# The attention gate folded into the output projection's weights, and the residual added where the partial projection is made

## The chip, the cores and the metric

The kernel runs on one core of a Trainium2 chip. The time is the device time of one execution in microseconds (us). The engines are TensorE (PE, with its weight loads listed apart as PEld), VectorE (DVE), ScalarE (ACT), GpSimd (POOL) and SyncE (SP). SP issues nearly all the DMA transfers, in its own order; an instruction on SP that must wait for a tile holds up everything behind it.

## The reference, cut to what matters

One encoder layer with 1024 positions, model width 1024, 8 latent-attention (MLA) heads and 8 chunked-attention heads of width 64, and a gated MLP of width 2816, all in float32. `g_a`, the attention gate, has one value for each output column and is the same for all positions.

```python
mod = jnp.dot(jax.nn.silu(c), w_ada[l]) + b_ada[l]
sh_a, sc_a, g_a, sh_m, sc_m, g_m = jnp.split(mod, N_MOD, axis=-1)
h = modulate(rmsnorm(x, g_attn_norm[l]), sh_a, sc_a)
...
o_mla = mla_attention(q, k, v)
...
o_ca = chunk_attention(cq, ck, cv, rel_bias[l])
mixed = jnp.dot(jnp.concatenate([o_mla, o_ca], axis=-1), w_out[l])
x = x + g_a[:, None, :] * mixed
h = modulate(rmsnorm(x, g_mlp_norm[l]), sh_m, sc_m)
u = causal_dwconv(jnp.dot(h, w_up[l]), conv_w[l], conv_b[l])
gate, val = jnp.split(u, 2, axis=-1)
x = x + g_m[:, None, :] * jnp.dot(jax.nn.silu(gate) * val, w_down[l])
```

## The kernel before

Every float32 operand of a large product is split into a high part (`hi_of`, line 77 when ACT makes it) and a low part (`lo_of`, line 84, a subtraction on POOL or DVE), and `gemm3` makes three matmuls of each pair: lines 154, 155 and 156. An engine letter chooses who splits: "a" is ACT, "p" POOL, "v" DVE.

The work runs in this order.

1. Up to about 400 us: the modulation vectors, the first norm, the input projection, and the chunked heads. Each head is a unit of four or eight query tiles. For each tile PE makes scores (L765 or L771), DVE masks and takes their minimum (the scores carry a minus sign; L789, L790), ACT exponentiates (L797), DVE takes the reciprocal of the sum (L799, L800), POOL makes a float16 high part (L73) and DVE the low part (L819), SP issues a transposing DMA (L831, tile `PTm` for the latent heads), and PE multiplies by the values (L859) into `pvm`. ACT and DVE together scale the result into `om` (L868, L869), and SP stores it to `oT_d` in DRAM (L873).
2. About 400 to 627 us: the latent heads, by the same steps. Between the tiles' matmuls other work is interleaved (`pace` and `fill_step` take it from the list `fillers`). The last filler is `f_oca`, the chunked heads' half of the output projection: it loads four 128x512 blocks of `w_out` for each half of the columns (`load_wo`), then for each of the 8 row tiles loads the heads' output `cl` and, for each half of the columns, runs 12 matmuls into a PSUM tile `oc`; ACT copies that into a tile `co` (L686; two buffers, tag "sq") and SP stores it to `part_d` (L687).
3. A side filler, `f_ada`, computes the remaining modulation vectors. It leaves the attention gate, spread over all 128 partitions, in DRAM as `ga_d`, long before `f_oca`.
4. About 627 to 722 us: the latent heads' half of the projection. For each row tile 24 matmuls go into `op` (two PSUM banks; three such tiles), with `oh` and `ol` (the heads' output, `o_load`) against `wo` (the other four blocks of `w_out`, from `load_wo` again). DVE then adds the partial sum (L1141), multiplies by the gate `gabc` (L1142), adds x (L1143); SP stores `x1_d`; ACT squares for the norm (L1145), POOL finishes the mean (L119, L120), DVE scales (L1150). PE transposes the rows (`mod_T`, L1044), ACT applies scale and shift (`hv`, L1046), and `bpage` and lines 1179 to 1199 make the differences and splits `b..` and `t..` that the MLP's products use (L1075, L1082 to L1084).
5. From about 722 us: the up-projection by a Strassen-like scheme, convolution, gate and down-projection, to the end at 1344 us.

The order of instructions on each engine is not that of the text: a planner in the framework simulates the program with its own costs and priorities and writes each engine's order (the heads have a high priority; `issue_after` adds constraints). So a change in the text also moves instructions it doesn't name. An engine executes its order strictly.

`load_wo` takes its raw tiles from a pool with tag "A" and five buffers (`atile`), shared with `f_ada`; a tile's buffer comes free when its last reader is done. For `f_oca` both halves are split by ACT and POOL. The late call is `wo = [load_wo(0, n, "a", "v" if n else "p") for n in range(2)]`: the second half's low parts are made by DVE.

Of the kernel before, what the change touches and what calls it, by code (L numbers as in the profile page):

```python
# [13 lines left out]
F32 = mybir.dt.float32  # L14
# [4 lines left out]
AF = mybir.ActivationFunctionType  # L19
# [3 lines left out]
MUL, ADD, SUB, MIN, MAX = ALU.mult, ALU.add, ALU.subtract, ALU.min, ALU.max  # L23

P = 128
D = 1024
# [38 lines left out]
def layer_kernel(ctx, tc, I, out):  # L65
    nc = tc.nc
    pe, act, dve, pool, sp = nc.tensor, nc.scalar, nc.vector, nc.gpsimd, nc.sync

    def f32(ap):
        return ap.bitcast(F32)  # L70
# [4 lines left out]
    def hi_of(eng, o, i):  # L75
        if eng == "a":
            act.activation(o, i, AF.Copy)  # L77
        elif eng == "p":
            pool.tensor_scalar(o, i, 1.0, 0.0, op0=MUL, op1=ADD)
        else:  # L80
            dve.tensor_copy(o, i)

    def lo_of(eng, o, i, hi):
        (pool if eng == "p" else dve).tensor_tensor(o, i, f32(hi), op=SUB)  # L84
# [4 lines left out]
    part_d = dram.tile([NT, P, D], F32, name="part_d")  # L89
    ga_d = dram.tile([P, D], F32, name="ga_d")  # L90
# [24 lines left out]
    anchor = {}  # L115

    def rsqrt_mean(r, ss, n, cols=None):
        sc = ss if cols is None else ss[:, cols]
        pool.tensor_scalar(sc, sc, 1.0 / n, EPS, op0=MUL, op1=ADD)  # L119
        anchor["r"] = pool.tensor_tensor(r, ss, nhalf[:].to_broadcast(list(r.shape)), op=ALU.pow).ins  # L120
# [17 lines left out]
    def rtile(name, shape=(P, 512), dt=F32):  # L138
        return apg.tile(list(shape), dt, name=name, tag="R", bufs=4)

    def qtile(name):
        return apg.tile([P, 512], F32, name=name, tag="sq", bufs=2)

    def atile(name):
        return apg.tile([P, 512], F32, name=name, tag="A", bufs=5)
# [4 lines left out]
    def gemm3(pt, pairs, start=True, stop=True):  # L150

        n = len(pairs)
        for i, (sh, sl, mh, ml) in enumerate(pairs):
            pe.matmul(pt, sh, mh, start=(start and i == 0), stop=False)  # L154
            pe.matmul(pt, sh, ml, start=False, stop=False)  # L155
            last = pe.matmul(pt, sl, mh, start=False, stop=(stop and i == n - 1))  # L156
        anchor["pe"] = last.ins
# [5 lines left out]
    def gemm3_f(pt, pairs, step=GSTEP):  # L163
        n, w = len(pairs), pt.shape[-1]
        for i0 in range(0, n, step):
            part = pairs[i0:i0 + step]
            if len(trail) > LAG:
                with tc.issue_after(trail[-1 - LAG]):
                    gemm3(pt, part, i0 == 0, i0 + step >= n)
            else:  # L170
                gemm3(pt, part, i0 == 0, i0 + step >= n)
            yield 3 * len(part) * max(107, w / 2.4 + 2.5)
# [104 lines left out]
    for d in range(ND):  # L277
# [7 lines left out]
        pt = ps.tile([P, 512], F32, name=f"p_ada{d}", tag="mm", bufs=2)  # L285
# [14 lines left out]
        for t in range(NT):  # L300
            h, j = divmod(t, 4)
            sl = slice(j * P, (j + 1) * P)
# [285 lines left out]
    def g4(shape, dt, name):  # L588
        return G["4"].tile(shape, dt, name=name, tag="G4", bufs=8)
# [71 lines left out]

    def load_wo(k0, n, he, le):
        ws = []
        for k in range(k0, k0 + 4):
            raw = atile(f"wor{k}_{n}")
            sl = slice(n * 512, (n + 1) * 512)
            sp.dma_start(raw[:], I["w_out"][k * P:(k + 1) * P, sl])
            w = g4([P, 2, 512], F32R, f"wo{k}_{n}")
            hi_of(he, w[:, 0], raw[:])
            lo_of(le, w[:, 1], raw[:], w[:, 0])  # L670
            ws.append(w)
        return ws

    def f_oca():
        ws = [load_wo(4, n, "a", "p") for n in range(2)]
        for t in range(NT):
            lo = rtile(f"cl{t}", (P, 4, P), F32R)
            hi = rtile(f"ch{t}", (P, 4, P), F32R)
            sp.dma_start(f32(lo[:]), oT_d[4:8, :, t * P:(t + 1) * P].rearrange("k p t -> p k t"))
            hi_of("a", hi[:], f32(lo[:]))  # L680
            lo_of("p", lo[:], f32(lo[:]), hi[:])
            for n in range(2):
                pt = ps.tile([P, 512], F32, name=f"oc{t}_{n}", tag="mm", bufs=2)
                yield from gemm3_f(pt[:], [(hi[:, k], lo[:, k], ws[n][k][:, 0], ws[n][k][:, 1]) for k in range(4)])
                o = qtile(f"co{t}_{n}")
                act.activation(o[:], pt[:], AF.Copy)  # L686
                sp.dma_start(part_d[t][:, n * 512:(n + 1) * 512], o[:])  # L687


# [322 lines left out]
    oh, ol, ox = {}, {}, {}  # L1012

    def o_load(t):
        ol[t] = go.tile([P, 4, P], F32R, name=f"ol{t}", tag="ol", bufs=4)
        oh[t] = go.tile([P, 4, P], F32R, name=f"oh{t}", tag="oh", bufs=4)
        anchor["ol"] = sp.dma_start(f32(ol[t][:]), oT_d[0:4, :, t * P:(t + 1) * P].rearrange("k p t -> p k t")).ins
        hi_of("a", oh[t][:], f32(ol[t][:]))
        lo_of("p", ol[t][:], f32(ol[t][:]), oh[t][:])
# [9 lines left out]
    gb = gbp.__enter__()  # L1029
# [11 lines left out]
    def mod_T(k, h):  # L1041
        pt = ps2.tile([P, 512], F32, name=f"ht_ps2_{k}_{h}", tag="hT", bufs=2)
        for j in range(4):
            pe.transpose(pt[:, j * P:(j + 1) * P], xn2[4 * h + j][:, k * P:(k + 1) * P], ident[:])  # L1044
        v = tb.tile([P, 512], F32, name=f"hv2_{k}_{h}", tag="v", bufs=13)
        act.activation(v[:], pt[:], AF.Identity, scale=modT[:, 2, k:k + 1], bias=modT[:, 3, k:k + 1])  # L1046
        return v

    def bpage(nm, k, v, le):
        pg = hpools[(nm, k)] if (nm, k) in hpools else h2p.tile([P, 2, 512], F32R, name=f"{nm}_{k}")  # L1050
        hi_of("a", pg[:, 0], v[:])
        lo_of(le, pg[:, 1], v[:], pg[:, 0])
        B[nm, k] = pg
# [1 line left out]
    r2 = cst.tile([P, NT], F32, name="r2")  # L1055
    xn2 = {}
    cvp = xp.tile([P, NC_PACK - C_CV], F32, name="cvp")
    gabc = gb.tile([P, D], F32, name="gabc")
    def mt(tag, shape, name, dt=F32):
        return mp["a" if tag in ("raw", "w2", "ws") else "b"].tile(list(shape), dt, name=name, tag=tag, bufs=MB[tag])  # L1060

# [47 lines left out]
        w.append(split(a12, f"wg{j}"))  # L1109
        return w  # L1110

    op_ = {t: gb.tile([P, D], F32, name=f"pa{t}", tag="pa", bufs=4) for t in range(4)}

    def x_load(t):
        if t > 3:
            op_[t] = gb.tile([P, D], F32, name=f"pa{t}", tag="pa", bufs=4)
        sp.dma_start(op_[t][:], part_d[t])
        if t not in ox:
            ox[t] = tb.tile([P, D], F32, name=f"x1_{t}", tag="x1", bufs=8)
        with tc.issue_after(anchor["ol"]):  # L1120
            anchor["wu"] = sp.dma_start(ox[t][:], I["x"][t * P:(t + 1) * P, :]).ins

    ox[7] = tb.tile([P, D], F32, name="x1_7", tag="x1", bufs=8)
    sp.dma_start(gabc[:], ga_d[:])
    for t in range(2):
        x_load(t)
    raw0, wa0, wb0 = ff_load(0)
# [5 lines left out]
    for t in range(NT):  # L1133
        pt = ps2.tile([P, 1024], F32, name=f"op{t}", tag="op", bufs=3)
        for n in range(2):
            gemm3(pt[:, n * 512:(n + 1) * 512],
                  [(oh[t][:, k], ol[t][:, k], wo[n][k][:, 0], wo[n][k][:, 1]) for k in range(4)])
        if t + 4 < NT:
            o_load(t + 4)
        pa, x1 = op_[t], ox[t]  # L1140
        dve.tensor_tensor(pa[:], pa[:], pt[:], op=ADD)  # L1141
        dve.tensor_tensor(pa[:], pa[:], gabc[:], op=MUL)  # L1142
        dve.tensor_tensor(x1[:], x1[:], pa[:], op=ADD)  # L1143
        sp.dma_start(x1_d[t], x1[:])
        act.activation(pa[:], x1[:], AF.Square, accum_out=ss2[:, t:t + 1])  # L1145
        if t + 4 < NT:
            x_load(t + 4)
        rsqrt_mean(r2[:, t:t + 1], ss2[:, t:t + 1], D)
        xn2[t] = x1
        dve.tensor_scalar(x1[:], x1[:], r2[:, t:t + 1], 1.0, op0=MUL, op1=MUL)  # L1150
        if t == 4:
            for k in range(ND):
                v0[k] = mod_T(k, 0)
                bpage("b11" if k < 4 else "b21", k % 4, v0[k], "v" if k % 2 else "p")
# [371 lines left out]
    for t in range(4):  # L1526
        o = dl.tile([P, 512], F32, name=f"oe{t}", tag="oe", bufs=3)
# [62 lines left out]
def build(arrays):  # L1590
    nc = bacc.Bacc("TRN2", target_bir_lowering=False, num_devices=1, dynamic_dma_scratch_size=1024)
    I = {k: nc.dram_tensor(k, v.shape, mybir.dt.from_np(v.dtype), kind="ExternalInput").ap()
         for k, v in arrays.items()}
    out = nc.dram_tensor("out_0_dram", (S, D), F32, kind="ExternalOutput").ap()
    with tile.TileContext(nc, schedule_with_timeline_sim=True) as tc, ExitStack() as ctx:
        layer_kernel(ctx, tc, I, out)
    return nc
# [8 lines left out]
```

## Time and profile before

| | us |
|---|---|
| median of 3 runs (lowest, highest) | 1341.02 (1340.53, 1343.16) |
| the profiled execution | 1345.89 |
| its span in the trace | 1344.1 |
| PE busy | 1223.8 |
| DVE busy | 1096.2 |
| ACT busy | 622.7 |
| POOL busy | 578.1 |

The mean granted TensorE clock of that execution is 0.946. In the rows quoted below, a group of instructions is written as line, engine, operation, output and inputs, shape and count, then the total busy time, the mean ns of one, and the idle time of the engine just before them with what ended most of it. A row of waits is the engine and line that waited, what it waited for, the total in us, how many times, and the longest. A row of windows has the stretch, its length, the busy time of each engine with the count of instructions, the granted clock (1.00 is full), the share of the DMA engines' time and the GB/s. Chain and timeline rows begin with start and duration. A tile's rows give the minimum, median and maximum ns of one instruction, and the starts of the first and the last.

### The profile page before, as it was taken

To read this page: it belongs to the slowest core of one execution; us is meant where nothing else is said; L and a number is where in the kernel's file an instruction comes from. 1 tells how busy PE (TensorE), PEld (TensorE's weight loads), DVE (VectorE), ACT (ScalarE), POOL (GpSimd) and SP (SyncE) were. 2 spreads that over 40 slices of the span, in tenths; PEclk is the share of its full clock that TensorE was granted. 3 is DMA by queue.
4 is the path that set the end of the run, shared out by engine and by line. 5 is a ranking of instruction groups with operands and counts; after the bars stand their busy time and mean duration, and the time that the engine had idled before them with its cause. 6 is when DMAs were issued, how large, how long until landed. Compare 5 with 4: busy or idle time off the path is not lost.

```text
span 1344.1 us, 18696 instructions
## 1 busy us (share of the span) xinstructions
PE 1223.8 (91%) x6168; PEld 1003.8 (75%) x6168; DVE 1096.2 (82%) x1928; ACT 622.7 (46%) x1132; POOL 578.1 (43%) x610
## 2 busy tenths in 40 slices
PE   4899798998877798886998999999999998999998
PEld 3788587896655567765776888888888886888886
DVE  6978798864679987894989988988899997687667
ACT  4453546443555544563376444444434444433431
POOL 5464557565646763354634444444445431000000
PEclk9899798998787889996999999999999998999999
DMA  8415577854413477779911333333323326943441
GB/s 323 138 35 116 135 177 179 192 127 110 87 32 80 94 153 165 141 150 252 377 49 47 126 110 133 103 122 98 133 102 118 126 98 241 390 141 117 130 161 63
DMA packets 223689, 190.57 MB, mean 142 GB/s; under 512 B 148708, under 2 KB 166884, under 8 KB 223592
## 3 DMA queue, kind: packets, MB, share of 16 engines
q1 hardware_dynamic: 223592, 189.38, 49.1%
q8 instruction: 48, 0.79, 0.2%
q14 instruction: 49, 0.40, 0.1%
HBM read 117.24 MB, written 37.49 MB: 115 GB/s over the span
## 4 chain that ended last, share of the span: by engine, by line
PE 41%; DVE 10%; issue 3%; ACT 2%; DMA 1%; POOL 1%; SPq 0%; DVEq 0%; ACTq 0%; POOLq 0%
PE p L1082 7%; PE p L1084 7%; PE p L1083 7%; PE dnA_P L1417 2%; PE dnA_P L1419 2%; PE dnA_P L1418 2%; PE dnB_P L1419 1%; PE dnB_P L1418 1%; PE dnB_P L1417 1%; DVE u L1253 1%; DVE u L1254 1%; PE op L154 1%; PE dnA L1417 1%; PE dnA L1419 1%; PE dnA L1418 1%
## 5 line engine op out<-in xcount | busy, mean ns | idle before, releaser
L77 ACT ACTIVATE dnP<-dnr 128x1024 fp32r<-128x1024 f32 x73 | 77.5, 1064 | 117.5 <-PE dnA_P L1419 46.4
L1391 DVE TENSOR_TENSOR dnP<-dnr,dnP 128x1024 fp32r<-128x1024 f32 x72 | 87.9, 1223 | 52.6 <-ACT dnP L77 52.6
L73 POOL TENSOR_SCALAR hlm<-Pm,rim 128x512 f16<-128x512 f32 (+3 forms) x96 | 68.8, 726 | 83.5 <-DVE rim L800 22.3
L84 POOL TENSOR_TENSOR wf<-wu,wf 128x512 fp32r<-128x512 f32 x22 | 38.8, 1762 | 116.3 <-ACT wf L77 116.3
L1253 DVE SCALAR_TENSOR_TENSOR u<-c,cvp,u 128x1023 f32<-128x1023 f32 x44 | 64.8, 1513 | 27.8 <-ACT u L1252 27.8
L73 POOL TENSOR_SCALAR hlc<-Pc,ric 128x640 f16<-128x640 f32 (+2 forms) x64 | 50.8, 797 | 61.0 <-ACT Pc L797 20.8
L819 DVE SCALAR_TENSOR_TENSOR hlm<-Pm,rim,hlm 128x512 f16<-128x512 f32 (+3 forms) x96 | 68.0, 719 | 9.8 <-POOL hlm L73 9.7
L797 ACT ACTIVATE Pc<-sc,mc 128x640 f32<-128x640 f32 (+2 forms) x64 | 42.1, 658 | 53.1 <-DVE mc L786 35.9
L797 ACT ACTIVATE Pm<-sm,mm 128x128 f32<-128x128 f32 (+3 forms) x64 | 47.1, 736 | 41.7 <-DVE mm L790 24.2
L84 POOL TENSOR_TENSOR wb<-wu,wb 128x512 fp32r<-128x512 f32 x22 | 38.1, 1732 | 64.5 <-ACT wb L77 50.7
L1252 ACT ACTIVATE u<-c,cvp 128x1024 f32<-128x1024 f32 x44 | 52.3, 1237 | 27.8 <-DVE c L1351 19.2
L1254 DVE SCALAR_TENSOR_TENSOR u<-c,cvp,u 128x1022 f32<-128x1022 f32 x44 | 63.8, 1488 | 0.0
L859 PE MATMUL pvm<-PTm,vt 128*128 128x256 f16 (+1 forms) x320 | 45.7, 294 | 17.0 <-DMA PTm<-hlm 9.9
L819 DVE SCALAR_TENSOR_TENSOR hlc<-Pc,ric,hlc 128x640 f16<-128x640 f32 (+2 forms) x64 | 51.6, 809 | 9.3 <-POOL hlc L73 8.7
L155 PE MATMUL ipq<-wq_s,hT 128*128 128x256 f32 x192 | 56.0, 292 | 0.1
L859 PEld LDWEIGHTS <-vt 128*128 128x128 f16 x320 | 31.6, 109 | 32.7 <-DMA PTm<-hlm 15.0
L154 PE MATMUL ipq<-wq_s,hT 128*128 128x256 f32 x192 | 55.8, 293 | 0.0
L156 PE MATMUL ipq<-wq_s,hT 128*128 128x256 f32 x192 | 55.4, 289 | 0.0
L77 ACT ACTIVATE wc<-ws 128x512 fp32r<-128x512 f32 x21 | 13.3, 632 | 88.0 <-DVE ws L1101 82.2
L1418 PE MATMUL dnA_P<-dnP 128*128 128x512 f32 x132 | 51.4, 389 | 0.0
L1419 PE MATMUL dnA_P<-dnP 128*128 128x512 f32 x132 | 51.3, 389 | 0.0
L1417 PE MATMUL dnA_P<-dnP 128*128 128x512 f32 x132 | 51.2, 389 | 0.0
(442 smaller groups left out, 4428.4 us busy)
## 6 DMA issues: line engine op xcount, KB each, us to landing
wu<-w_up SPq DMA_DIRECT2D x44, 512.0 KB, 3.5
dnr<-g_d SPq DMA_DIRECT2D x73, 256.0 KB, 2.8
aw<-w_ada SPq DMA_DIRECT2D x48, 256.0 KB, 3.5
g_d<-u SPq DMA_DIRECT2D x22, 512.0 KB, 3.0
dnr<-w_down SPq DMA_DIRECT2D x44, 256.0 KB, 5.3
adaw<-w_ada_a SPq DMA_DIRECT2D x16, 512.0 KB, 6.3
x<-x SPq DMA_DIRECT2D x16, 512.0 KB, 9.0
g_d<-gs SPq DMA_DIRECT2D x22, 256.0 KB, 2.8
```

Of the source, the lines that this page charges most:

```text
L73: pool.tensor_scalar(o, i, s, 1.0, op0=MUL, op1=MUL)
L77: act.activation(o, i, AF.Copy)
L797: act.activation(pr[:, :n], sv, AF.Exp, bias=m[:], scale=-1.0, accum_out=rsum[:, 0:1])
L819: dve.scalar_tensor_tensor(hl[:, w:2 * w], pp, ri[:], hl[:, :w], op0=MUL, op1=SUB)
L1082: pe.matmul(pt, sh, pg[:, 0], start=(k == 0 and not add), stop=False, skip_group_check=skip)
L1083: pe.matmul(pt, sh, pg[:, 1], start=False, stop=False, skip_group_check=skip)
L1084: last = pe.matmul(pt, sl, pg[:, 0], start=False, stop=(k == 3), skip_group_check=skip)
L1253: dve.scalar_tensor_tensor(u[:, 1:], c[:, :S - 1], cvp[:, cv + 1:cv + 2], u[:, 1:], op0=MUL, op1=ADD)
L1391: r = f(*a, **k)
L1417: pe.matmul(pt, sh, w[:, 0, 0], start=start, stop=False, skip_group_check=add)
L1418: pe.matmul(pt, sh, w[:, 1, 0], start=False, stop=False, skip_group_check=add)
L1419: pe.matmul(pt, sl, w[:, 0, 0], start=False, stop=stop, skip_group_check=add)
```

## The change

- `load_wo` loads the matching 128x512 piece of the gate, `ga`, from `ga_d` into the same pool as the raw blocks, and multiplies each raw block by it in place, before the split. POOL does it where it also makes the low parts (12 blocks), DVE for the other four.
- `f_oca` loads the matching 128x512 piece of x into `co` ahead of the matmuls. Instead of ACT's copy, DVE adds the PSUM tile `oc` to it. What is stored to `part_d` is then x plus the gated partial projection.
- At the end, the tile `gabc` with its load and the tiles `pa` with their eight loads are gone. `x1` is loaded from `part_d` instead of x, and one DVE addition of `op` replaces the three passes. ACT's square writes its unused elementwise output to a small tile of its own, `xj2`, with two buffers.

```diff
     def load_wo(k0, n, he, le):
         ws = []
+        sl = slice(n * 512, (n + 1) * 512)
+        ga = atile(f"ga{k0}_{n}")
+        sp.dma_start(ga[:], ga_d[:, sl])
         for k in range(k0, k0 + 4):
             raw = atile(f"wor{k}_{n}")
-            sl = slice(n * 512, (n + 1) * 512)
             sp.dma_start(raw[:], I["w_out"][k * P:(k + 1) * P, sl])
+            (pool if le == "p" else dve).tensor_tensor(raw[:], raw[:], ga[:], op=MUL)
             w = g4([P, 2, 512], F32R, f"wo{k}_{n}")
             hi_of(he, w[:, 0], raw[:])
             lo_of(le, w[:, 1], raw[:], w[:, 0])
...
             for n in range(2):
+                o = qtile(f"co{t}_{n}")
+                sp.dma_start(o[:], I["x"][t * P:(t + 1) * P, n * 512:(n + 1) * 512])
                 pt = ps.tile([P, 512], F32, name=f"oc{t}_{n}", tag="mm", bufs=2)
                 yield from gemm3_f(pt[:], [(hi[:, k], lo[:, k], ws[n][k][:, 0], ws[n][k][:, 1]) for k in range(4)])
-                o = qtile(f"co{t}_{n}")
-                act.activation(o[:], pt[:], AF.Copy)
+                dve.tensor_tensor(o[:], o[:], pt[:], op=ADD)
                 sp.dma_start(part_d[t][:, n * 512:(n + 1) * 512], o[:])
...
-    gabc = gb.tile([P, D], F32, name="gabc")
...
     def x_load(t):
-        if t > 3:
-            op_[t] = gb.tile([P, D], F32, name=f"pa{t}", tag="pa", bufs=4)
-        sp.dma_start(op_[t][:], part_d[t])
         if t not in ox:
             ox[t] = tb.tile([P, D], F32, name=f"x1_{t}", tag="x1", bufs=8)
         with tc.issue_after(anchor["ol"]):
-            anchor["wu"] = sp.dma_start(ox[t][:], I["x"][t * P:(t + 1) * P, :]).ins
+            anchor["wu"] = sp.dma_start(ox[t][:], part_d[t]).ins
...
-    sp.dma_start(gabc[:], ga_d[:])
...
-        pa, x1 = op_[t], ox[t]
-        dve.tensor_tensor(pa[:], pa[:], pt[:], op=ADD)
-        dve.tensor_tensor(pa[:], pa[:], gabc[:], op=MUL)
-        dve.tensor_tensor(x1[:], x1[:], pa[:], op=ADD)
+        x1 = ox[t]
+        dve.tensor_tensor(x1[:], x1[:], pt[:], op=ADD)
         sp.dma_start(x1_d[t], x1[:])
+        pa = gb.tile([P, D], F32, name=f"xj2_{t}", tag="xj2", bufs=2)
         act.activation(pa[:], x1[:], AF.Square, accum_out=ss2[:, t:t + 1])
```

More of the change, by code (lines that the diff above doesn't have):

```diff
@@ L1110, in ff_sums @@
         return w
-    op_ = {t: gb.tile([P, D], F32, name=f"pa{t}", tag="pa", bufs=4) for t in range(4)}
     def x_load(t):
-        if t > 3:
-            op_[t] = gb.tile([P, D], F32, name=f"pa{t}", tag="pa", bufs=4)
-        sp.dma_start(op_[t][:], part_d[t])
         if t not in ox:
```

## The prediction

> **What bounds the kernel now.** I read the page's busy times first, then the windows by stage, and then, in the two stages that the change touches, the waits of each engine and the chain.
>
> ```profile
> span 1344.1 us, 18696 instructions
> PE 1223.8 (91%) x6168; PEld 1003.8 (75%) x6168; DVE 1096.2 (82%) x1928; ACT 622.7 (46%) x1132; POOL 578.1 (43%) x610
> core 0: us, PE busy (x) PEld busy (x) DVE busy (x) ACT busy (x) POOL busy (x), PEclk, DMA share, GB/s
> 400.00:480.00 80.00, 57.81 (x267) 44.46 (x267) 75.18 (x222) 46.03 (x109) 57.02 (x57) 0.77 0.43 93
> 480.00:600.00 120.00, 109.06 (x625) 86.67 (x626) 99.78 (x258) 61.66 (x129) 53.17 (x69) 0.97 0.74 152
> 600.00:627.00 27.00, 17.41 (x94) 12.58 (x94) 18.13 (x40) 10.19 (x21) 13.32 (x16) 0.78 0.82 183
> 627.00:678.00 51.00, 47.95 (x203) 38.70 (x201) 37.97 (x28) 17.58 (x31) 32.41 (x27) 0.92 0.93 350
> 678.00:722.00 44.00, 37.85 (x186) 29.23 (x184) 40.54 (x57) 33.60 (x57) 12.14 (x8) 1.00 0.04 18
> ```
>
> PE is the busiest over the whole span, but the averages hide stages. In 400–480 DVE binds (75.18 of 80). In 480–600, where the latent heads run with the chunked heads' half of the projection as filler, PE has 11 us idle and DVE 20. In 600–627 nothing is full: a stage of latencies. From 627 to 722, the late projection and the norm behind it, PE is busy 85.8 of 95, so 9.2 us is all that any relief of another engine can return there, unless the clock changes.
>
> ```profile
> PE c_g L1083 <- DVE b L84: 2.5, 2, 1.6
> PE op L154 <- ACT oh L77: 2.5, 1, 2.5
> PE p L1075 <- DVE t L84: 2.3, 1, 2.3
> PE ht_ps L1044 <- ACT hv L1046: 0.8, 1, 0.8
> PE c_g L1083 <- POOL b L84: 0.7, 1, 0.7
> PE op L156 <- POOL ol L84: 0.6, 1, 0.6
> ```
>
> These are PE's waits from 627 to 723 (total, times, longest): 9.4 us, of which 4.8 us end on DVE and 2.5 us stand at the start of the late projection.
>
> **The change part by part.**
>
> *The end.* Three DVE passes per 128x1024 tile become one.
>
> ```profile
> L1143 DVE TENSOR_TENSOR x<-x,pa 128x1024 f32<-128x1024 f32 x8 | 14.8, 1848 | 0.2
> L1142 DVE TENSOR_TENSOR pa<-pa,gabc 128x1024 f32<-128x1024 f32 x8 | 12.7, 1588 | 0.2
> L1141 DVE TENSOR_TENSOR pa<-pa,op 128x1024 f32<-128x1024 f32 x8 | 9.7, 1214 | 11.8 <-PE op L156 11.8
> DMA to landing us min/median/max: 5.9/7.8/10.0
> 692.11 0.69 DVE L1179 TENSOR_TENSOR hv<-hv,hv 128x512 f32<-128x512 f32 x1 [1.02 <-ACT hv L1046]
> 720.82 1.89 DVE L84 TENSOR_TENSOR t<-hv,t 128x512 fp32r<-128x512 f32 x3
> ```
>
> What stays is the L1141 form (8 of 1.21 us, one operand in PSUM); L1142 and L1143 go, 12.7 + 14.8 = 27.5 us of DVE. It is not 27.5 us of time: behind L1141 DVE already sat 11.8 us waiting for PE, so up to the last matmul of the late projection the removal mostly lengthens that idle. What counts is the backlog at the hand-over. The chain of one tile from its last matmul to its scaled row is shortened by L1142 and L1143, some 2 x 1.2 to 2 x 2.3 = 2.4 to 4.6 us. Then DVE has its own run from 692.11 to 722.7 (692.11, to the last split at 720.82 + 1.89), without a pause over 1.5 us: about 30 us of differences and splits that end in the operand PE waits 2.3 us for. In the changed order that run starts 4 to 5 us earlier against the projection's start and keeps its length, so PE recovers its two DVE waits (2.5 + 2.3) less what becomes late next: ACT's hv copies (0.8) and POOL's splits (0.7), which were just behind DVE. I take 3.5 of the 4.8. The eight loads of part_d and the gate's load (4.5 MB) also go; they run at a DMA share of 0.93, but none of the waits above ends on a transfer, so I cost that at 0. The cover is the earlier issue of the x1 loads; without it the first add would be late, by no more than the 7.8 us median landing of the present pa loads (the landing row above is theirs), and that lies in the range's upper end only.
>
> *The start of the late projection.* Order written by the planner: the changed program issues the last two w_out loads eight or nine SP transposes earlier, and ACT makes the first three oh tiles before the last head's output.
>
> ```profile
> 623.35 0.57 SPq L667
> 623.97 3.90 DMA wor<-w_out
> 624.06 3.38 PE L859 MATMUL pvm<-PTm,vt 128*128 128x256 f16 x16 [3.38 <-DMA PTm<-hlm]
> 627.90 0.63 ACT wo L77
> 628.55 0.68 ACT om L868
> 629.25 0.64 ACT oh L77
> 629.94 0.79 PE op L154
> ```
>
> Now the chain runs load, split, om, oh, matmul, while PE's last values end at 624.06 + 3.38 = 627.44: the 2.50 us to 629.94 go. Tail: -3.5 - 2.5 = -6.0. Bounds: -9.4 (every wait above) and -2.5 (only this one).
>
> *The adds in the filler.* Sixteen ACT copies become sixteen DVE adds of 128x512, one operand in PSUM, and sixteen loads of x into co are issued by SP.
>
> ```profile
> L686 ACT ACTIVATE co<-oc x16: 577/592/598, 490.2 to 609.4; 128x512 f32<-128x512 f32 x16
> L687 SPq DMA_DIRECT2D part_d<-co x16: 319/531/572, 491.8 to 610.6; - x16
> DMA to landing us min/median/max: 2.1/2.4/3.6
> 734.36 0.68 DVE L1337 TENSOR_TENSOR c<-c,p 128x512 f32<-128x512 f32 x1
> ACT co L686 <- PE oc L156: 8.8, 6, 3.4
> ACT Pm L797 <- DVE mm L790: 18.1, 12, 3.5
> ACT Pm L797 <- DVE rim L800: 9.0, 5, 2.8
> PE sm L771 <- ACT Pm L797: 4.2, 5, 1.7
> SPq L831 <- DVE hlm L819: 12.7, 10, 3.3
> ```
>
> The nearest row to the add is L1337, same shape and operands: 0.68. So DVE gets 16 x 0.68 = 10.9 us where its idle is 20 us in 480–600. ACT loses 16 x 0.59 = 9.4 us, worth nothing: ACT itself waits 18.1 + 9.0 us for DVE's minima and normalisers, and PE's scores wait 4.2 us for ACT's exponentials. So this moves work from the engine that waits to the engine that is waited for, in the order minimum (L790), exponential (L797), reciprocal (L799), split (L819), SP transpose (L831), values. The 8.8 us that ACT stood at L686 for the last matmul of oc now stand on DVE, and behind them the next minimum. A second wait is new: the load of co. There are two co slots, and in the changed order the loads of co2_0, co2_1, co3_0, co6_0 and co7_1 come two to four SP instructions behind the store that frees their slot; store 2.4 us, load about the same (2.4 to 3.6), two issues of 0.53: some 6 to 8 us from one add to the next in a slot, where DVE has 4 to 5 us of other work between. That is 2 to 3 us on DVE for each of about two such places. SP itself stands about 1 us at each for the slot, in front of transposes. Against it: the planner placed the adds, and where the idle DVE time and the add fall together they are free. I count half the adds (5.4) as time, 2.5 for load stalls and 1 for SP: +9, less the holes that now stand in DVE's waits for POOL and PE, 3: +6. Bounds: -2 (ACT's relief counts, all adds in holes) and +16 (10.9 + 5).
>
> *The gate in the weights.* Sixteen multiplies of 128x512 and four loads of the gate, 256 KB.
>
> ```profile
> L84 POOL TENSOR_TENSOR wo<-wor,wo x12: 1260/1422/1730, 409.6 to 604.6; 128x512 fp32r<-128x512 f32 x12
> L84 DVE TENSOR_TENSOR wo<-wor,wo x4: 673/692/693, 606.8 to 628.6; 128x512 fp32r<-128x512 f32 x4
> 328.99 0.25 POOL L465 TENSOR_TENSOR lat<-lat,tabk 128x32 f32<-128x32 f32 x1 [10.85 <-ACT lat L481]
> L1142 DVE TENSOR_TENSOR pa<-pa,gabc x8: 1216/1226/2329, 640.5 to 679.9; 128x1024 f32<-128x1024 f32 x8
> ```
>
> Twelve go to POOL at about the price of its split (1.42): 17 us. Four stand in the 10.85 us hole before 328.99 (5.7 of it): 0. Five at 415–440 and three at 465–485, where POOL is busy 57 of 80: mostly holes, but POOL is in the softmax chain (L73 before L819), and DVE with two SBUF operands is stretched beside POOL. L1142 shows that: one form, 1.22 to 2.33 us. In a stage in which DVE has 5 us left I put +1.5 (0 to 5). The four DVE multiplies, 4 x 0.69 = 2.8, fall into 606–627, where DVE is idle 9 of 27: +0.5. The atile pool has five slots; a call now takes all five, so the next call's loads wait for the former call's lo splits. POOL therefore makes wo0_0 and wo1_0 before the last head's hlm, and SP's loads of wor0_1 and wor1_1 wait for that in front of the last transposes: a hop of POOL's 1.4 us or two, in a stage where nothing hides it. I put no more than +0.5 beside the gain above (bounds 0 and 4). The four gate loads cost SP 4 issues of about 0.5 (L687's), beside its transposes: 0.
>
> The Trainium skill, "SBUF — State Buffer", section "Who interferes with whom", says that a DVE instruction with two SBUF inputs contends with a GpSimd instruction that reads SBUF, one of them blocking fully, and one with at most one SBUF input does not. The rows of L1141 (PSUM operand, 1.21) and L1142 agree. By it the new adds would keep 0.68, and each POOL multiply beside a two-operand DVE instruction would block by up to its own length, 8 x 1.42 = 11 at the very most instead of my 1.5.
>
> Sum: -6.0 + 6 + 1.5 + 0.5 + 0.5 = +2.5; the chained hops of 600–627, where each late link is paid in full, make it +3.5 by adding 1 for one more POOL or DVE link of that size. The profiled execution took 1345.89 (span 1344.1 and 1.8 around it), 4.9 above the median of 1341.02; the change is taken from the one and added to the other: 1341.0 + 3.5 = 1344.5.
>
> **The rivals.** *A, faster:* DVE's adds fall into its 20 us of idle time and the tail's gain stands whole. For it: PE, the busiest engine, gets not one instruction more, and its waits on ACT in 480–600 are only 4.2. Against it: the order puts adds between minimum and split. Then -6 to -9 and +1 to +2: about 1336. It decides if less than 5 us is lost ahead of 627. The Trainium skill, "Perfetto Trace Analysis", section "Optimization Strategy", says that with regimes of different bounds interleaving them can help; moving 27.5 us out of the DVE-bound run behind 678 into a PE-bound stage is such a move, and it speaks for this rival. *B, the stall is larger:* each co load that is late holds DVE, DVE holds the chain, and SP's waits for the slot hold transposes that are already late (12.7 us behind L819). Five such places at 2 to 3 us: +12 instead of +6, with the rest as above +10: 1351. For it: two slots only; against it: most adds are well apart. *C, the tail's bound is not removed:* DVE's run from 692 starts with the transposes of mod_T, so it may be set by PE and ACT and keep its place; then only the 2.5 goes, and the sum is +7: 1348.
>
> **How the numbers follow.** My forecast (1342 to 1349) 0.38, A (1330 to 1340) 0.34, B (1349 to 1357) 0.20, C (1346 to 1350) 0.08. The range leaves out the far tails of A and B: 1332 to 1354. Within 0.2% (2.7 us, about what the runs can tell from no change) lie the lower fifth of the forecast (0.08) and the edge of A (0.03): same 0.11, faster 0.31, slower 0.58.
>
> **What would show it.** PE's wait for oh at the first op matmul gone or under 1 us; DVE's last split of t some 5 us nearer to that matmul; PE busy in 627–722 near 86 of 89. Before it: the last pvm matmul ending near 637 instead of 627.4, waits of DVE for co loads of 2 to 6 us, adds of 0.68. Wrong if the last pvm ends before 632 (A), or if those waits exceed 8 us (B), or if the stretch from the first op matmul to the late product is as long as now (C).

## The result and the profile after

The changed kernel takes 1359.06 us (median of 4 runs, 1358.28 to 1361.52) where the kernel before takes 1341.36 (median of 4): ratio 1.0131, 95% interval 1.0112 to 1.0149, 17.7 us slower. The forecast was 1344.5 within 1332 to 1354: the direction was right, the size was too small by a factor of five, and the time lies outside the range.

The profiled execution of before that the prediction works with was a long one for this kernel (1345.89). A second one, taken later of the same kernel, took 1341.51 (span 1339.7), close to the median; the first runs 3.8 us behind it from 485 us on. From here on "before" in a trace is this second execution. The changed kernel's profiled execution took 1358.32 (span 1356.5), 0.7 below its median. So the traces differ by 16.8 us and the medians by 17.7.

The page and the windows of the changed kernel:

```profile
span 1356.5 us, 18703 instructions
PE 1222.7 (90%) x6168; PEld 1007.0 (74%) x6168; DVE 1080.3 (80%) x1932; ACT 615.6 (45%) x1116; POOL 584.4 (43%) x622
480.00:600.00 120.00, 101.08 (x555) 81.23 (x556) 92.75 (x238) 48.32 (x103) 47.17 (x61) 0.93 0.77 170
600.00:648.00 48.00, 30.80 (x162) 23.05 (x161) 35.48 (x78) 18.39 (x36) 22.21 (x26) 0.82 0.81 177
648.00:698.00 50.00, 50.00 (x233) 41.44 (x233) 18.11 (x18) 22.54 (x39) 26.49 (x31) 1.00 0.71 258
```

The same for before, second execution:

```profile
480.00:600.00 120.00, 109.19 (x631) 86.57 (x632) 101.16 (x257) 64.01 (x136) 56.63 (x73) 0.99 0.74 155
600.00:626.00 26.00, 14.95 (x81) 10.67 (x79) 16.04 (x34) 9.82 (x18) 9.28 (x11) 0.74 0.91 193
626.00:676.00 50.00, 48.52 (x209) 38.75 (x210) 38.38 (x29) 17.33 (x32) 33.16 (x29) 0.97 0.89 345
```

Over the span DVE is busy for 20 us less in the changed kernel than in the kernel before (1080.3 against 1100.6 in its second execution), ACT for 6 us less (615.6 against 621.8), PE for 3 us more (1222.7 against 1219.9) and POOL for 6 us more (584.4 against 578.1). In 480–600 every compute engine does less in the same 120 us: PE falls from 109 to 101 us, DVE from 101 to 93. The stage did not get more work than an engine can hold; its chain got longer. The stage that ends with the last `pvm` matmul ends 24 us later, and the late projection behind it is better off: there PE has no idle time and the full clock, while DVE's work halves.

Where PE waits, first before and then after. The first row of each fence is PE's wait for the transposes (tile `PTm`), total and times; the timeline rows are the last `pvm` matmuls and the first of `op`.

```profile
  PE pvm L859: 13.6, 10
620.24 3.38 PE L859 MATMUL pvm<-PTm,vt 128*128 128x256 f16 x16 [3.36 <-DMA PTm<-hlm]
626.10 0.50 PE L154 MATMUL op<-wo,oh 128*128 128x512 f32 x1 [2.48 <-ACT oh L77]
```

```profile
  PE pvm L863: 28.6, 16
644.57 3.38 PE L863 MATMUL pvm<-PTm,vt 128*128 128x256 f16 x16 [5.97 <-DMA PTm<-hlm]
647.71 0.58 PE L154 MATMUL op<-wo,oh 128*128 128x512 f32 x1
```

PE's wait for the transposed probabilities doubles, 13.6 to 28.6 us. That is a form in which the loss shows here and not its cause: with the old order held (below) the whole change loses more, and this wait is 12.4 us. The 2.48 us ahead of the first `op` matmul are gone. From the first `op` matmul to the end, before needs 1339.7 - 626.1 = 713.6 and the changed kernel 1356.5 - 647.7 = 708.8: the tail gained 4.8 us. Ahead of it 21.6 us were lost (647.7 against 626.1). In nine traces of kernels with the old end (those of the kernel before and of seven runs below), the stretch from the first `op` matmul on takes 713.0 to 718.0 us, so the gain there is more than the spread of executions.

### The profile page after: what moved, and what is told of

Its sections match the earlier page's. It is cut to its first block, busy times and chain, and to the rows that moved or that the text cites. A ratio compares the mean times of both kernels' runs of the same rounds, so it can differ in the third digit from the quotient of the medians.

```text
span 1356.5 us, 18703 instructions
## 1 busy us (share of the span) xinstructions
PE 1222.7 (90%) x6168; PEld 1007.0 (74%) x6168; DVE 1080.3 (80%) x1932; ACT 615.6 (45%) x1116; POOL 584.4 (43%) x622
## 4 chain that ended last, share of the span: by engine, by line
PE 42%; DVE 8%; issue 3%; ACT 2%; DMA 1%; POOL 0%; DVEq 0%; SPq 0%; ACTq 0%; POOLq 0%
PE p L1085 7%; PE p L1087 7%; PE p L1086 7%; PE dnA_P L1413 2%; PE dnA_P L1415 2%; PE dnA_P L1414 2%; PE dnB_P L1415 1%; PE dnB_P L1414 1%; PE dnB_P L1413 1%; DVE u L1250 1%; DVE u L1249 1%; PE op L154 1%; PE op L156 1%; PE op L155 1%; PE dnA L1413 1%
## 5 line engine op out<-in xcount | busy, mean ns | idle before, releaser
L73 POOL TENSOR_SCALAR hlm<-Pm,rim 128x512 f16<-128x512 f32 (+2 forms) x96 | 70.7, 746 | 84.8 <-DVE rim L804 36.4
L1249 DVE SCALAR_TENSOR_TENSOR u<-c,cvp,u 128x1023 f32<-128x1023 f32 x44 | 61.0, 1426 | 27.6 <-ACT u L1248 26.2
L863 PE MATMUL pvm<-PTm,vt 128*128 128x256 f16 (+1 forms) x320 | 46.4, 296 | 32.6 <-DMA PTm<-hlm 28.6
L823 DVE SCALAR_TENSOR_TENSOR hlm<-Pm,rim,hlm 128x512 f16<-128x512 f32 (+2 forms) x96 | 67.7, 715 | 6.5 <-POOL hlm L73 6.2
L1250 DVE SCALAR_TENSOR_TENSOR u<-c,cvp,u 128x1022 f32<-128x1022 f32 x44 | 59.6, 1393 | 0.0
L823 DVE SCALAR_TENSOR_TENSOR hlc<-Pc,ric,hlc 128x640 f16<-128x640 f32 (+2 forms) x64 | 52.1, 817 | 9.2 <-POOL hlc L73 8.8
```

Of the source, the lines that this page charges most:

```text
L73: pool.tensor_scalar(o, i, s, 1.0, op0=MUL, op1=MUL)
L823: dve.scalar_tensor_tensor(hl[:, w:2 * w], pp, ri[:], hl[:, :w], op0=MUL, op1=SUB)
L863: last = pe.matmul(dst, u.vst(j), mov, start=(x == 0), stop=(x == len(todo) - 1), skip_group_check=True)
```

## The experiments

All medians stand against runs of the kernel before on the same chip in the same session (1341.9 to 1343.2). A difference in us below is the ratio less 1, times 1342. In a table:

| kernel | median us | ratio (95%) |
|---|---|---|
| gate half, free order | 1350.39 | 1.0057 (1.0036 to 1.0078) |
| x half, free order | 1348.55 | 1.0048 (1.0034 to 1.0063) |
| copies on DVE, free order | 1344.55 | 1.0018 (1.0000 to 1.0036) |
| loads of x alone, free order | 1353.82 | 1.0091 (1.0064 to 1.0118) |
| changed, x loaded by ACT's queue | 1352.10 | 1.0078 (1.0057 to 1.0100) |
| tiny multiplies | 1347.52 | 1.0055 (1.0035 to 1.0074) |
| gate in the late weights only | 1348.19 | 1.0057 (1.0032 to 1.0081) |
| changed, five co buffers | 1355.21 | 1.0104 (1.0089 to 1.0119) |
| 16 free POOL writes | 1339.69 | 0.9972 (0.9959 to 0.9985) |
| the end alone | 1339.97 | 0.9973 (0.9949 to 0.9996) |
| partial sum added ahead | 1344.24 | 1.0008 (0.9995 to 1.0022) |
| before again | 1342.27 | 1.0003 (0.9979 to 1.0027) |
| gate half, order held | 1356.40 | 1.0096 (1.0072 to 1.0121) |
| x half, order held | 1356.23 | 1.0100 (1.0083 to 1.0118) |
| whole change, order held | 1367.12 | 1.0192 (1.0174 to 1.0209) |
| copies on DVE, order held | 1349.51 | 1.0054 (1.0036 to 1.0073) |
| loads of x on SP, order held | 1354.99 | 1.0086 (1.0058 to 1.0113) |
| loads of x on ACT, order held | 1350.48 | 1.0052 (1.0027 to 1.0076) |

The line of the 16 free writes is also a measure of what this table can tell. That kernel issues every instruction of the kernel before in the same order and adds 16 POOL writes of 0.1 us, which ran in the first 4 us, and came out 0.28% faster. So differences under about 4 us are not told apart here, whatever their interval. Single traces spread as much: the two executions of the kernel before reach the first `op` matmul at 626.1 and 629.9 us.

**One half at a time.** The gate half:

```diff
+        ga = atile(f"ga{k0}_{n}")
+        sp.dma_start(ga[:], ga_d[:, sl])
...
+            (pool if le == "p" else dve).tensor_tensor(raw[:], raw[:], ga[:], op=MUL)
...
-        dve.tensor_tensor(pa[:], pa[:], gabc[:], op=MUL)
```

> Only the gate is moved into the weights; f_oca is as before, and at the end the partial sum and x are still added in two passes (only the multiplication by the gate is gone). Theory S (the loss of the change comes from SP: 16 loads of x, about 0.5 us of SP each plus waits for a co slot, stand among the transposes, 1.24 us of SP each): the multiplies are nearly free, 1337 to 1344. Theory D (the loss comes from 16 adds on DVE instead of ACT): the same, 1337 to 1344. Theory G (the loss comes from the gate's multiplies and the slots of the atile pool): 1350 or more.

Measured: 1350.39. The x half (the rest of the change):

> Only the addition of x is moved; the gate is left out altogether, so this kernel does no multiplication by it, neither in the weights nor at the end. Theories S and D: most of the loss is here, 1352 to 1360. Theory G: 1332 to 1343, the tail's gain without the loss.

Measured: 1348.55. Neither half is free: +7.6 and +6.4 us. No single theory of the three holds. Both have a gain at the end inside them, so their costs in the attention stage are larger than these: the last `pvm` matmul starts at 639.0 us in the trace of the gate half and at 633.6 in that of the x half, against 623.3 before and 647.6 with the whole change. That is 15.7 and 10.3 us, and 24.3 for both together.

**The two ingredients of the x half.** Copies on DVE:

```diff
-                act.activation(o[:], pt[:], AF.Copy)
+                dve.tensor_copy(o[:], pt[:])
```

> The kernel before with one edit: the 16 copies of oc into co are made by DVE instead of ACT; no load of x. Theory D: 1347 to 1356, most of the loss without any load. Theory S: 1339 to 1345.

Measured: 1344.55. Loads alone:

```diff
+                o = qtile(f"co{t}_{n}")
+                sp.dma_start(o[:], I["x"][t * P:(t + 1) * P, n * 512:(n + 1) * 512])
                 pt = ps.tile([P, 512], F32, name=f"oc{t}_{n}", tag="mm", bufs=2)
...
-                o = qtile(f"co{t}_{n}")
                 act.activation(o[:], pt[:], AF.Copy)
```

> The kernel before with one edit: co is first loaded with x by SP, and ACT's copy then overwrites it, so the loads and their waits for a slot are there and DVE has nothing more to do. Theory S: 1349 to 1358. Theory D: 1341 to 1345. With S and D each holding half, this one and the copy on DVE each show about half of the loss.

Measured: 1353.82. The loads cost 12 us without an add on DVE; the copies on DVE cost 2.4 (0 to 4.8) without a load, which is not told apart from nothing. Here theory S looked settled; the runs with a held order below show that it was not.

**The loads of x: another queue, more buffers.**

```diff
-                sp.dma_start(o[:], I["x"][t * P:(t + 1) * P, n * 512:(n + 1) * 512])
+                act.dma_start(o[:], I["x"][t * P:(t + 1) * P, n * 512:(n + 1) * 512])
```

> The changed kernel, with the 16 loads of x into co issued by ACT instead of SP; nothing else in the text. If the x half of the loss (7 to 11 us) is SP's time in front of the transposes, this kernel is faster than the changed one by that: 1348 to 1353. If it is DVE's adds or their wait for the loaded tile, it stays at 1356 to 1362.

```diff
-                o = qtile(f"co{t}_{n}")
+                o = atile(f"co{t}_{n}")
```

> The changed kernel with the co tiles taken from the pool of five buffers that lies idle between the two loads of w_out, instead of the pool of two: SP no longer waits for the store of an earlier co (5.1 us in the changed kernel), and loads can be issued early; the 16 issues stay. If SP's waits for a slot are the x half: 1350 to 1354. If the 16 issues of 0.5 us themselves, or DVE's adds: 1356 to 1360.

Measured: 1352.10 and 1355.21. Taking the loads from SP returns about 7 of the 17.7 us, in an order that the planner wrote anew. Five buffers instead of two return about 4, at the limit of what is told apart and between the two forecasts. They did not do away with the waits for a slot: SP still waits 3.6 us for the store of an earlier `co` (5.1 in the changed kernel), so this run doesn't rule on those waits.

**The gate half: dependency, place, planner.** Tiny multiplies, 128x2 by ones in the place of the gate's:

```diff
+            (pool if le == "p" else dve).tensor_tensor(raw[:, :2], raw[:, :2], ones[:, :2], op=MUL)
```

> The kernel before with 16 multiplies of 128x2 by ones where the changed kernel multiplies 128x512 by the gate (the gate stays at the end). There is next to no work in them and no load of the gate, but the planner orders a program with one more step in each split. If the gate half of the loss (8 us) is work, loads and buffers: 1340 to 1344. If it comes from the other order that the planner writes for a program with such a step: 1347 or more.

Measured: 1347.52, as much as the whole gate half with next to none of its work. The gate in the late weights alone:

```diff
+        ga = None if k0 else atile(f"ga{k0}_{n}")
...
+            if ga is not None:
+                (pool if le == "p" else dve).tensor_tensor(raw[:], raw[:], ga[:], op=MUL)
...
-        dve.tensor_tensor(pa[:], pa[:], pt[:], op=ADD)
         dve.tensor_tensor(pa[:], pa[:], gabc[:], op=MUL)
         dve.tensor_tensor(x1[:], x1[:], pa[:], op=ADD)
+        dve.tensor_tensor(x1[:], x1[:], pt[:], op=ADD)
```

> The gate goes into the late weights alone (8 multiplies and 2 loads of the gate just ahead of the late projection); the chunked heads' half is gated and added to x at the end, ahead of the late matmuls' results, so that one DVE pass is left behind them. If the gate half is lost in the multiplies and slots of the late call: 1346 to 1352. If it is lost in the early call, with the tail's gain of about 5: 1335 to 1341.

Measured: 1348.19. By the forecast that is the late call: its last `pvm` matmul starts 7.5 us later than before (630.8 against 623.3). It doesn't clear the early call, whose cost with the order held is shown below. From the first `op` matmul to the end this kernel gains next to nothing (713.0 against 713.6), though only one DVE pass stands behind each result. Sixteen POOL writes into a tile that nobody reads:

```diff
+            pool.memset(idle[:], 1.0)
```

> The kernel before with 16 POOL writes of 128x2 into a tile that nobody reads, one for each raw block of w_out. No dependency, no load and next to no work (some 0.1 us each). If the loss with the 128x2 multiplies (5.7) came from POOL and DVE waiting for the raw blocks in their queues: 1340 to 1343. If any edit at this place makes the planner write an order that is some us worse: 1345 to 1349.

Measured: 1339.69. The planner wrote the same order as for the kernel before, so this did not test what another order costs. The tiny multiplies did get another one (some 370 of PE's 6168 matmuls stand elsewhere in its trace). Either that order or the wait of POOL and DVE for each raw block, in front of what is queued behind them, costs their 7 us; in its trace POOL waits 8.5 us and DVE 6.7 for the raw blocks at the multiplies, and these runs don't say which.

**The end.** The end of the change alone:

```diff
-        dve.tensor_tensor(pa[:], pa[:], pt[:], op=ADD)
-        dve.tensor_tensor(pa[:], pa[:], gabc[:], op=MUL)
-        dve.tensor_tensor(x1[:], x1[:], pa[:], op=ADD)
+        dve.tensor_tensor(x1[:], x1[:], pt[:], op=ADD)
```

> Only the end of the change: one DVE addition of op to x, no load of part_d, no gate. It leaves the chunked heads' partial sum and the gate out. The stage ahead of it is as before. My prediction's tail term: -6.0, so 1333 to 1338. If the tail's relief is worth less because the splits behind it keep their place: 1338 to 1341.

Measured: 1339.97, a gain of 3.6 (0.5 to 6.8), no more than that of the 16 free writes. The trace says more than the median: from the first `op` matmul to the end it takes 709.0 us, where the nine with the old end take 713.0 to 718.0. One pass moved ahead, none saved:

```diff
-        dve.tensor_tensor(pa[:], pa[:], pt[:], op=ADD)
         dve.tensor_tensor(pa[:], pa[:], gabc[:], op=MUL)
+        dve.tensor_tensor(x1[:], x1[:], pa[:], op=ADD)
+        dve.tensor_tensor(pa[:], pt[:], gabc[:], op=MUL)
         dve.tensor_tensor(x1[:], x1[:], pa[:], op=ADD)
```

> Same result as the kernel before, another order at the end: the partial sum is gated and added to x ahead of the late matmuls' result, where DVE waits for PE, so that two DVE passes of 128x1024 stand behind the result instead of three; one pass more in all. If the relief behind the result is what counts: 1337 to 1341. If DVE's whole time counts: 1343 to 1347.

Measured: 1344.24, no difference. From the first `op` matmul to the end, its trace takes 713.9 us with four passes in all, two of them behind the result. The late weights alone took 713.0 with three and one, the gate half 709.5 with two and two. That points to the DVE work taken out of the stretch, and not to the number of passes behind a result, as what shortens it; these are single traces. And the second profile:

> The kernel before once more, for a second profiled execution of it: the first took 4 us more than the median of its runs. Its median should be within 0.2% of the other runs of the kernel before, and its stages show which of the differences of single profiles are only the spread of executions.

Measured: 1342.27.

**The order held.** Nearly all runs above mix an edit's work with the other order that the planner writes for it. So each shared instruction was tied behind its predecessor in the kernel before by an order-only edge, which waits for nothing; what the edit adds finds its own place, and in the gate half so do the loads of `w_out`, whose slots come free later.

```python
for e, seq in ORDER.items():          # the engine's order in the kernel before
    prev = None
    for k in seq:
        i = base[e][k]
        if i is None or i.name in FREE:
            continue
        if prev is not None:
            tc.add_manual_dep(i, prev.name, NO_SYNC, reason="pin")
        prev = i
```

> The gate half (gate in the weights, only its multiplication gone at the end), with every instruction that it shares with the kernel before held in the order of the kernel before by order-only edges; the multiplies and the loads of the gate and of w_out alone find their own place. Free order: 1350.4, 8 above before. Theory P (the gate half's loss is the planner's other order of the attention stage): 1338 to 1343. Theory W (multiplies, loads and buffers cost it whatever the order): 1347 to 1352.

> The x half (loads of x into co, adds on DVE, one pass at the end; the gate is left out altogether), all shared instructions held in the order of the kernel before. Free order: 1348.6, 6 above before. Theory S (16 loads on SP in front of the transposes): the loads are there in this order too, so 1346 to 1352. Theory P: 1336 to 1341, the tail's gain alone.

> The whole change, all shared instructions held in the order of the kernel before except the loads of w_out. Free order: 1359.1, 17 above before. Theory P: 1337 to 1343. Theories S and W: 1352 to 1360. With P for the gate half and S for the x half: 1346 to 1351.

> The 16 copies of oc on DVE instead of ACT, all shared instructions held in the order of the kernel before; no load of x. Free order: 1344.6, 2 above before. My prediction's term for DVE's adds (half of 10.9, less holes): about +3, so 1343 to 1347. If DVE's idle time takes them: 1340 to 1343.

Measured: 1356.40, 1356.23, 1367.12 and 1349.51. Theory P falls: with the order held, the gate half costs 12.9, the x half 13.4 and the whole change 25.8, more than in the free order (7.6, 6.4, 17.6; for the gate half the two intervals just touch). The halves add up (26.3 against 25.8). So the added work itself costs, in the places where the planner put it in this order, and for the whole change the planner's new order returned about 8 us rather than losing any. The copies on DVE, 16 of 0.68 = 10.9 us of DVE, cost 7.2 (4.8 to 9.8):

```profile
L686 DVE COPY co<-oc x16: 670/681/692, 488.8 to 615.9; 128x512 f32<-128x512 f32 x16
```

How a multiply on POOL costs time is seen in the rows at the first latent heads. POOL of before, then of the gate half with its order held:

```profile
413.81 2.53 POOL L84 TENSOR_TENSOR wo<-wor,wo 128x512 fp32r<-128x512 f32 x2
416.31 1.00 POOL L73 TENSOR_SCALAR hlm<-Pm,rim 128x512 f16<-128x512 f32 x1
```

```profile
326.49 1.28 POOL L670 TENSOR_TENSOR wor<-wor,ga 128x512 f32<-128x512 f32 x1 [2.32 <-DMA wor<-w_out]
327.79 0.25 POOL L465 TENSOR_TENSOR lat<-lat,tabk 128x32 f32<-128x32 f32 x1
414.49 1.26 POOL L84 TENSOR_TENSOR wo<-wor,wo 128x512 fp32r<-128x512 f32 x1
415.71 4.96 POOL L670 TENSOR_TENSOR wor<-wor,ga 128x512 f32<-128x512 f32 x4
420.62 1.27 POOL L84 TENSOR_TENSOR wo<-wor,wo 128x512 fp32r<-128x512 f32 x1
421.88 0.99 POOL L73 TENSOR_SCALAR hlm<-Pm,rim 128x512 f16<-128x512 f32 x1
```

The first four multiplies end inside the hole ahead of 327.8, for nothing, as forecast. The next four stand 4.96 us in front of the high part of a softmax tile; that starts 5.6 us later than before (421.88 against 416.31), and the first latent head's output is 5.3 us late (432.4 against 427.2) and never catches up. By the fourth output it is 9.3 us late (491.4 against 482.1). Three more multiplies lie in between, at 470.9 to 482.9, but the two executions of the kernel before differ by 2.6 us over the same stretch, so how much of these 4 us is theirs is not shown. The largest step is that of the late call, 6.8 us between the thirteenth and the fourteenth output (600.0 to 626.1 us, before 588.5 to 607.7). SP's loads and DVE there:

```profile
615.60 1.86 SPq L669 DMA_DIRECT2D wor<-w_out  x4
619.04 1.43 DVE L670 TENSOR_TENSOR wor<-wor,ga 128x512 f32<-128x512 f32 x2 [4.91 <-DMA wor<-w_out]
```

DVE stands 4.91 us at a multiply because the loads go out only from 615.60 on, and the low part of a softmax tile is queued behind it. That is a wait and not the multiply's length; the changed kernel in its free order has no such wait of DVE.

The loads, with the order held:

> The kernel before with co first loaded with x by SP and then overwritten by ACT's copy; every instruction of the kernel before keeps its order on its engine, 16 loads on SP are all that is added. Free order: 1353.8. Theory S: 16 issues of 0.5 us (8.5 us by the rows of the changed kernel) and a few waits for a slot stand in front of the transposes: 1349 to 1356. If the loads fall into SP's pauses: 1341 to 1345.

> The same kernel with the same 16 loads issued by ACT instead of SP, all else in the order of the kernel before. If what costs is SP's time in front of the transposes: 1341 to 1346, most of the loss of the SP form gone. If it is the traffic of the loads or the wait of ACT's copy for them, it stays within 3 us of the SP form.

Measured: 1354.99 and 1350.48: 11.5 us with SP issuing, 7.0 with ACT issuing. Their intervals overlap (7.8 to 15.2 and 3.6 to 10.2), so that SP's time is a part of it is likely and not shown; some 7 us stay when SP issues none of the loads. The trace of the SP form is that of its fastest execution, 6.3 us below its median, so its rows show how time is lost and not how much. The mechanism on SP is visible, though. SP before, and with the 16 loads on it:

```profile
506.54 1.35 SPq L687 DMA_DIRECT2D part_d<-co  x2
507.95 0.45 SPq L679 DMA_DIRECT2D cl<-oT_d  x1
508.50 3.80 SPq L831 DMA_TRANSPOSE PTm<-hlm  x2
```

```profile
505.70 0.86 SPq L688 DMA_DIRECT2D part_d<-co  x1
506.62 2.34 SPq L684 DMA_DIRECT2D co<-x  x2
510.25 0.33 SPq L688 DMA_DIRECT2D part_d<-co  x1
510.62 0.43 SPq L679 DMA_DIRECT2D cl<-oT_d  x1
511.15 1.22 SPq L832 DMA_TRANSPOSE PTm<-hlm  x1
  DMA co<-x: 9.2, 3
```

Before, the transpose starts at 508.50; with the loads, SP issues two of them, has to wait for ACT's copy before the next store, and the transpose starts at 511.15, though this execution had been 0.8 us ahead a moment earlier (505.70 against 506.54). The last row is ACT's own wait for the loaded tile, 9.2 us in three places: with two `co` tiles, a load can only go out when the store ahead of it has landed (SP waited 2.6 us for that, in three places). ACT's queue is in the softmax chain as well.

On the issuing engine, the Trainium skill ("DMA: Bandwidth & Descriptors", section "Issuing engines are not separate DMA queues") says that starting DMAs from several engines only saves the sequencer's time to start them, usually small beside the DMA. Here that time is not small beside what the queue has to do: a transpose holds SP for 1237 ns (median) and a load for 479, and the 7 us returned in the free order are of the size of 16 such loads (7.7).

## Why the prediction was right or wrong

- *The start of the late projection* (-2.5): right. ACT makes its first three `oh` tiles ahead of the last head's output (641.1 to 648.7 us), and PE's 2.48 us wait for `oh` is gone. What was not forecast is the clock granted there, 1.00 in 648–698 against 0.97 in 626–676.
- *The DVE term at the end* (-3.5): near in size, partly by luck. The trace shows -4.8 from the first `op` matmul to the end. DVE's last split of `t` ends 86.2 us after the first `op` matmul (733.9 - 647.7) where it was 92.2 (718.3 - 626.1): 6 us nearer, 5 were forecast. But the two waits of PE that the term was made of did not go away. In the fence, DVE's scaling before, then the changed kernel:

```profile
L1150 DVE TENSOR_SCALAR x<-x,r 128x1024 f32<-128x1024 f32 x8 | 8.9, 1110 | 0.9 <-DMA x_d<-x 0.9
L1138 DVE TENSOR_TENSOR x<-x,op 128x1024 f32<-128x1024 f32 x8 | 9.7, 1216 | 8.3 <-DMA x<-part_d 4.9 <-PE op L156 3.3
L1146 DVE TENSOR_SCALAR x<-x,r 128x1024 f32<-128x1024 f32 x8 | 6.6, 820 | 22.5 <-DMA x_d<-x 22.1 <-ACT b L77 0.5
PE p L1078 <- DVE t L84: 2.6, 2, 2.3
PE c_g L1086 <- DVE b L84: 2.0, 1, 2.0
```

  Nearly all of the freed 27.5 us of DVE became one wait, 22.1 us of the in-place scaling for the store of the same tile to `x1_d`; before, with two more passes in between, that wait was 0.9. And PE still waits for `t` and `b`, 4.6 us in all where it was 4.8. PE's first matmul on `t` stands 75.4 us after the first `op` matmul instead of 81.6. It waits for DVE there both times, so DVE's earlier end is a cause, as forecast. What the working lacked is that PE itself comes earlier, by no longer waiting for ACT and POOL (2.2 us) and because about as many matmuls take less time (355 in 73.4 us, before 353 in 77.0). So the waits that were to shrink stayed, and the total was near all the same.
- *The attention stage* (+6 for the adds and loads, +1.5 and +0.5 for the multiplies, +0.5 for the slots, +1 for the hops: +9.5): this is the step that failed. The last `pvm` matmuls end 24 us later (647.9 against 623.6), not 9.5. Two terms were mis-sized, in the free order. The gate's multiplies and slots, +2.5, cost 7.6 and what that kernel gains at the end besides. The loads of x, +3.5 (2.5 for DVE's waits and 1 for SP), cost 12 by themselves. The adds were put at 5.4 less 3 for holes, +2.4, and the copies on DVE cost 2.4 in the free order, so that term was not the one at fault there; with the order held it is 7.2.
- One assumption runs through these terms, "the holes that now stand in DVE's waits" and POOL "mostly holes": idle time of an engine was taken as room. With the order held, 10.9 us of DVE copies cost 7.2, and 5 us of POOL multiplies in front of one softmax tile cost 5.3. These engines are idle in short waits within a chain that goes through all of them in turn; of what is added in front of a link, two thirds (the copies) to all (the multiplies) was paid. The one hole that took work for nothing was that ahead of 328 us, outside the chain. The term for the slots, +0.5, was too small in the held order, where the late call has a wait of 4.9 us.
- *The loads of x*: I counted 2.5 for DVE's waits and 1 for SP's. DVE's waits were 2.6, as forecast, and SP's for a slot 5.1; but the loads alone cost 12. I priced DVE's stall for a late tile and left out that each issue holds a queue in front of transposes; the profile's page doesn't show SP's share of time, because issuing instructions aren't counted there. By the two runs with ACT issuing, that queue's part would be some 4 to 7 us; this is likely and not shown.
- *The adds' price*, 0.68 each: right, 0.686 (median). The Trainium skill's rule in "SBUF — State Buffer", section "Who interferes with whom", agrees: with one operand in PSUM they took 666 to 689 ns, none stretched. Its other half, that multiplies on POOL stretch DVE, is not what cost the time: the low parts L823 of the latent heads took 67.7 us in all, as L819 did before, and from 400 us to the first `op` matmul DVE's busy time grew by 11.5 us (193.4 to 204.9), less than the 13.7 of its own adds and multiplies.

```profile
L823 DVE SCALAR_TENSOR_TENSOR hlm<-Pm,rim,hlm 128x512 f16<-128x512 f32 (+2 forms) x96 | 67.7, 715 | 6.5 <-POOL hlm L73 6.2
L690 DVE TENSOR_TENSOR co<-co,oc x16: 666/686/689, 492.9 to 628.7; 128x512 f32<-128x512 f32 x16
```

- *The rivals.* A fell with the last `pvm` matmul 24 us later, not less than 5; its hidden adds fail with the order held (7.2) and are not settled in the free order (2.4). C (the tail's bound stays) is refuted by the trace of the end. B had the right sign and the nearest time (1351), but its decisive point, DVE's waits for loads above 8 us, did not come (2.6): the loads cost in another way, most likely through the queues.
- *What stays open*: which part of the 12 us of the loads is SP's time, which the wait for one of two slots and which ACT's; whether the tiny multiplies lose by their waits or by the planner's order; why the new order that the planner wrote for the whole change returns 8 us; and what the added work would cost in other places than those the planner chose. No version here beats the kernel before by more than the runs can tell: the end alone, the part of the change that gains, is worth 3.6 us.

## What to carry to other kernels

Idle time of an engine is room only if the work put there is not in front of a link of the chain that sets the end: look at what stands next in that engine's queue, and when a stage runs through all engines in turn, price an added instruction at up to its full length unless a hole outside the chain is shown. Count the queue that issues the DMAs as an engine, with the duration of each issue, and ask what is queued behind it. Where a planner orders the program, hold the old order once to tell the work from the order, and run a kernel with the same order twice to learn what a difference must exceed.

## What was not expected of the hardware

A transposing DMA holds SP for 1167 to 2251 ns (median 1237) in the second execution of the kernel before, against 0.3 to 0.6 us for most plain ones; 61 of them and 31 others fill 104 of the 120 us from 480 to 600, waits between them included. Two executions of one kernel can differ by 4 us that are lost in one stage: the first profile of before is 1.2 us behind the second at its first head output (427 us) and 3.7 behind at its fourth (482 us), and keeps that distance to the end.
